# Attention's output projection: weights loaded and split ahead, its last column tile held back, the last LayerNorm moved into the MLP's streams

## The chip, the cores and the metric

The kernel runs on one core of a Trainium2 chip. The metric is device time in microseconds (us) of one execution. The time before is the median of three runs. The profile is that of one more execution, whose own time is given below beside its span (from its first to its last instruction).

## What is computed

Two post-norm transformer layers over 1024 latent tokens and 256 context tokens of width 1024, all in fp32. Layer 0 is a retention and gated-linear-attention mixer, layer 1 a windowed attention; each ends in a squared-ReLU MLP. The change lies in layer 1. Cut to that:

```python
q, k, v = split_cols(h @ w, (ATT_QW, ATT_KVW, ATT_KVW))        # 16 query heads, 4 key/value heads, width 64
q, k = axial_rope(q), axial_rope(k)
# each block of 128 queries: a softmax over the keys with |i-j| <= 128, all 256 context keys and a sink logit
y = merge_heads(window_attention(q, k, v, k_c, v_c, od_sink[j])) @ od_w_out[j]     # the output projection
x = layer_norm(ALPHA * x + g1 * y)                                                # over the 1024 features
x = layer_norm(ALPHA * x + g2 * (relu((x * (1 + sc2) + sh2) @ mlp_w1) ** 2 @ mlp_w2))
```

## The kernel before

Activations lie with features on the 128 partitions and tokens in the free dimension; `accs[1]` and `accs[2]` hold 512 latent tokens each, as eight tiles of 128 features. A product in fp32 is made of three matmuls of halves (`mm3`): weight and activation are each split into a rounded high part and a low remainder, and high*high, high*low and low*high are summed in PSUM.

A weight is split by `wsplit` (L246 to L253): SP's queue loads a 128x1024 fp32 tile `raw` (three buffers), ACT casts it to the high part (L251), and POOL, or DVE where `eng` says so, subtracts to get the low part (L252). The pair lies in one tile of the tag `w`, of which the pool `wg` has five.

Attention is a loop over 32 groups `u`: eight query blocks `n`, four key/value heads `g`, each with four query heads. For one head, `scores` (L1353 on) writes the scores into one of two PSUM tiles `pS`; DVE takes the row maximum (L1381, L1382) and ACT the exponentials `E` with their sums (L1385). `dens` makes the reciprocals of the denominators and puts them on diagonals `dg` (POOL, L1398). `turn` transposes the E of four heads for one key block on PE into one of two PSUM tiles `pE`, and copies them to `Et` (ACT at L1410, DVE at L1408 for the third key block); the tile of the first four `Et` is of the tag `w` too. `pv` sums E times v into `pO`, `end` multiplies the denominators in (L1429, L1430) and splits the result into `yh` (ACT, L1432) and `yl` (DVE, L1433). A group has five key blocks inside the sequence and four at its two ends. The loop is a software pipeline: while the E of group `u` are turned, the scores of group `u+1` are made.

The output projection of a finished pair of blocks (256 tokens) is the generator `residual`, which calls `w_out_steps` (L746 on): eight column tiles, each with one weight pair, 24 matmuls into the single PSUM tile `pW`, and one DVE update of `accs` (L758). With `halves` it yields after 12 and after 24 matmuls. The loop advances it twice in a group, so that a column tile falls into each group from `u` = 8 on: first half after the second turn, second half after the last scores. `wsplit` is called where the first half begins. The projection of the last two blocks (t = 9) comes after the loop, in whole column tiles into `pE`, with POOL and DVE taking turns at the subtractions. `norm` is the LayerNorm of a finished stretch of 256 tokens, advanced once per group; it shares `pW` (its mean stays there for the four subtractions of L712). After the projections for t = 7 and t = 9, `make_h` writes the modulated, split MLP input of 256 tokens of `accs[1]` into `yall`, over the attention output that was just used. `residual` also loads 1 MB of the stream into `accs` by SP's queue, behind a small POOL copy (L1324, L1325).

The last stretch, `accs[2][:, :, 256:512]`, has its LayerNorm `ln_` as a generator of ten steps. Nine of them run before the MLP; the tenth, and the four steps of the MLP input made from it, are the second stream of `Early`, which `mlp` advances after each up and each down product of its first weight block, by the rates given to `Early`; `need` runs a stream dry where the MLP reads it.

Order: within attention, PE's instructions of the loop are chained in program order (`TE.kept`), except `end` of the last group, the norms and what follows the loop. All else is ordered by a planner that simulates the program and takes, for each engine, what is ready with the earliest place in the program; so a cast can stand on ACT earlier than in the program. Each engine then works through its list in order.

Of the kernel before, what the change touches and what calls it, by code (L numbers as in the profile page):

```python
# [9 lines left out]
F32 = mybir.dt.float32  # L10
F32R = mybir.dt.float32r
# [3 lines left out]
ALU = mybir.AluOpType  # L15
# [4 lines left out]
P = 128  # L20
KT = 8
T = 1280
NT = 10
# [11 lines left out]
def backbone(ctx: ExitStack, tc: tile.TileContext, xT, cin, wmod, bmod, lng, lnb, w1, w2,  # L35
# [4 lines left out]
    def pool(**kw):  # L40
        if kw.get("space") is not DRAM:
            kw["reuse_waits"] = "tile"
        return tc.tile_pool(**kw)

    V, S, G, SY = nc.vector, nc.scalar, nc.gpsimd, nc.sync
# [27 lines left out]
    rawp = ctx.enter_context(pool(name="rawp", bufs=3))  # L73
# [5 lines left out]
    def nm(s):  # L79
        uid[0] += 1  # L80
        return f"{s}_{uid[0]}"
# [149 lines left out]
    def adv(gen, n):  # L231
        for _ in range(n):
            if next(gen, "end") == "end":
                return
# [11 lines left out]
    def wsplit(pool, src, eng=None):  # L246
        raw = rawp.tile([P, 1024], F32, tag="raw", name=nm("raw"))
        SY.dma_start(raw, src)
        both = pool.tile([P, 2, 1024], F32R, tag="w", name=nm("w"))
        hi, lo = both[:, 0, :], both[:, 1, :]  # L250
        S.copy(hi, raw)  # L251
        (eng or G).tensor_tensor(lo, raw, hi.bitcast(F32), ALU.subtract)  # L252
        return hi, lo  # L253
# [8 lines left out]
    def mm3(pt, wh, wl, xh, xl, start, stop):  # L262
        TE.matmul(pt, lhsT=wh, rhs=xh, start=start, stop=False)
        TE.matmul(pt, lhsT=wh, rhs=xl, start=False, stop=False)
        TE.matmul(pt, lhsT=wl, rhs=xh, start=False, stop=stop)
# [24 lines left out]
    def first_load(q):  # L290

        raws = []
        for k in range(0, KT, 2):
            raw = b1.tile([P, 2, 2, 256], F32, tag=("E0", "Ei0", "E1", "Ei1")[k // 2], name=nm("raw"), bufs=1)
            for a in range(2):
                SY.dma_start(raw[:, a], wmod[0, (k + a) * P:(k + a + 1) * P, 0:2048]
                             .rearrange("p (b c) -> p b c", b=2)[:, :, q * 256:q * 256 + 256])
            raws.append(raw)
        return raws
# [31 lines left out]
    def t16(name):  # L331
        return b1.tile([P, 16], F32, tag=name, name=name, bufs=1)
    u = t16("u")
# [24 lines left out]
    raws = first_load(0)  # L358
# [26 lines left out]
    with es_b1:  # L385
# [20 lines left out]
        for q in range(4):  # L406
            first_mods(q, raws)
            x_ = xs
            if q < 3:
                raws = first_load(q + 1)  # L410
# [138 lines left out]
    wg = ctx.enter_context(pool(name="wg", bufs=5, side="right"))  # L549
# [196 lines left out]
    def w_out_steps(y, wsrc, wp, acc, l, j, pW, engs=(None, None), wnext=None, halves=False):  # L746

        n = acc.shape[2]
        yh, yl = y
        for u in range(KT):  # L750
            wh, wl = [w.rearrange("p (k m) -> p k m", k=KT) for w in (wnext() if wnext else wsplit(wp, wsrc[u], engs[u % 2]))]
            pt = pW()
            for k in range(KT):
                xh, xl = [y_[k // 4][:, k % 4, :] if isinstance(y_, list) else y_[:, k, :] for y_ in (yh, yl)]
                mm3(pt[:, :n], wh[:, k, :], wl[:, k, :], xh, xl, k == 0, k == KT - 1)
                if halves and k == 3:
                    yield
            V.scalar_tensor_tensor(acc[:, u, :], pt[:, :n], gta[:, l, 0, u, j:j + 1], acc[:, u, :],  # L758
                                   op0=ALU.mult, op1=ALU.add)
            yield  # L760
# [5 lines left out]
    pSc, pO, pR, pW, pL = ring(2, 3), ring(0, 1), ring(4), ring(5, 7), ring(6)  # L766
# [9 lines left out]
    with pool(name="b3", bufs=1) as b3:  # L776
# [32 lines left out]
        def wnext():  # L809
            while len(ahead) <= n_ahead:  # L810
                src = next(srcs, None)
                if src is None:
                    break
                ahead.append(wsplit(wg, *src))
            return ahead.pop(0)
# [27 lines left out]
        def out_of(p_, y):  # L843
            return w_out_steps(y, wo0, wg, acc_of(p_)[0], 0, acc_of(p_)[1], pW, wnext=wnext)
# [31 lines left out]
        for tp_ in range(NT // 2):  # L876
# [20 lines left out]
            for t in (2 * tp_, 2 * tp_ + 1):  # L897
# [21 lines left out]
                for h in range(4):  # L919
                    en = V  # L920
# [91 lines left out]
        end = out_of(NT // 2 - 1, (yh, yl))  # L1012
# [106 lines left out]
    def new_h(hp, ci, l, mp, os_=(0, 256), los=(V, G)):  # L1119

        if ci not in hs:
            hs[ci] = h_tiles(hp, ci)
        return [((ci, o), h_steps(accs[ci][:, :, o:o + 256], l, 1, cj(ci), hs[ci][0][:, :, o:o + 256],
                                  hs[ci][1][:, :, o:o + 256], mp, "hf", 2, los=los)) for o in os_]

    es_h = ExitStack()
    hp = es_h.enter_context(pool(name="hp0", bufs=1))
    xd = [dram(f"xd{c}", [P, KT, CH[c][1]]) for c in range(3)]
    with pool(name="m0", bufs=1) as mp:
        ln_ = layer_norm_steps(accs[2][:, :, 256:512], 0, 0, mp, "ln_s", "ln_q", 1, True, pL, 512)  # L1130
        early = Early([new_h(hp, 1, 0, hp, (0,), (V, V)) + new_h(hp, 1, 0, hp, (256,)) + new_h(hp, 2, 0, hp, (0,)), [(None, ln_)] + new_h(hp, 2, 0, hp, (256,))], ((2, 2), (2, 2)))
# [38 lines left out]
        rest = mlp(0, [0, 1, 2], hs, accs, wg, mp, post, chain(*[mod_sums(1, s_, mp, pM) for s_ in range(3)]), tick, ticks0, early)  # L1170
# [24 lines left out]
    pS, pE, pO, pW = bank2("S2", 1024, 2), bank2("E2", 512, 2), bank2("O2", 512, 1), bank2("W2", 512, 1)  # L1195
# [38 lines left out]
    todo = None  # L1234
    for grp in range(3):
# [19 lines left out]
        for i in range(4):  # L1255
            src = wkv[i] if grp == 0 else wq[4 * (grp - 1) + i]
            wu.append(wsplit(wg, src, V if i % 2 else G))
        for t in range(0 if grp == 0 else 2, NT):
# [30 lines left out]
            todo = nxt  # L1289
# [14 lines left out]
    with pool(name="p2", bufs=1) as p2:  # L1304
# [3 lines left out]
        def get_v(t):  # L1308
            if t not in vts:
                v_ = p2.tile([P, 256], F32, tag="vc" if t < 2 else "vl", name=nm("v"), bufs=2 if t < 2 else 4)  # L1310
                SY.dma_start(v_, vTd[t])
                vts[t] = v_
            return vts[t]
# [2 lines left out]
        G.memset(ones_c, 1.0)  # L1316
        get_v(0)
        get_v(1)
        def residual(y, t, ci):
            o0 = (t - 1) * P - CH[ci][0]  # L1320
            if o0 == 0:
                accs[ci] = new_acc(acp, ci)
            asl = accs[ci][:, :, o0:o0 + 256]
            G.tensor_copy(asl[:, 0, 0:1], first[0])  # L1324
            SY.dma_start(asl, xd[ci][:, :, o0:o0 + 256])  # L1325
            yield from w_out_steps(y, wo1, wg, asl, 1, 0, pW if t < NT - 1 else pE, (None, None) if t < NT - 1 else (None, V), halves=t < NT - 1)
            if t in (NT - 3, NT - 1):
                make_h(accs[1][:, :, o0:o0 + 256], 1, 1, 0, *[y_[:, :, o0:o0 + 256] for y_ in yall], p2, "ln_q", 1)

# [8 lines left out]
        rest, norms = iter(()), iter(())  # L1338
# [98 lines left out]
        todo = [(n, g) for n in range(8) for g in range(4)]  # L1437
# [5 lines left out]
        for u, (n, g) in enumerate(todo):  # L1443
            nk, _, dens, turn, pv, end = nxt
            nxt = group(*todo[u + 1]) if u + 1 < len(todo) else None
            dens()
            for kk in range(nk):
                turn(kk)
                if nxt and kk < 3:
                    nxt[1](kk)  # L1450
                if kk == 1:
                    adv(rest, 1)
            if nxt:
                nxt[1](3)
            adv(rest, 1)
            for kk in range(nk):
                pv(kk)
            end()
            TE.kept = False
            adv(norms, 1)  # L1460
            TE.kept = u + 1 < len(todo)
            if g == 3 and n % 2 == 1:
                adv(rest, 1000)
                if n > 1:
                    adv(norms, 1000)
                    norms = norm(n, chunk_of(n))
                rest = residual([y_[:, :, (n % 4) * P - P:(n % 4) * P + P] for y_ in yall], n + 2, chunk_of(n + 2))
        for _ in rest:
            adv(norms, 1)
        adv(norms, 1000)  # L1470
    if stop == "x3":
# [10 lines left out]
    with pool(name="hp1", bufs=1) as hp, pool(name="m1", bufs=1) as mp:  # L1482
        hs = {1: yall}
        ln_ = layer_norm_steps(accs[2][:, :, 256:512], 1, 0, mp, "ln_s", "ln_q", 2, True, pL, 512, True)
        early = Early([new_h(hp, 2, 1, mp, (0,)), [(None, ln_)] + new_h(hp, 2, 1, mp, (256,))], ((4, 4), (4, 4)))
        adv(ln_, 9)

        pend = []

        def post(ci, o0, n):  # L1490
            c0 = CH[ci][0] - 256 + o0

            def store(k, kn):
                (SY if k % 4 else S).dma_start(out[:, k:k + kn, c0:c0 + n], accs[ci][:, k:k + kn, o0:o0 + n])

            g_ = layer_norm_steps(accs[ci][:, :, o0:o0 + n], 1, 1, mp, "ln_s", "ln_q", 2, True, pL, 512, store)
            while next(g_) != "free":
                pass
            while pend:
                adv(pend.pop(), 100)  # L1500
            pend.append(g_)

        post(*mlp(1, [1, 2], hs, accs, wg, mp, post, early=early))
        adv(pend.pop(), 100)
# [102 lines left out]
```

## Time and profile before

| | |
|---|---|
| median of 3 runs | 3048.98 us (3047.06 to 3050.82) |
| the profiled execution's own time | 3047.85 us |
| its span | 3046.1 us |
| PE (TensorE, matmuls) busy | 2871.2 us, 94% of the span |
| PE's weight loads busy | 2414.7 us, 79% |
| DVE (VectorE) busy | 1660.5 us, 55% |
| ACT (ScalarE) busy | 981.1 us, 32% |
| POOL (GpSimd) busy | 811.0 us, 27% |
| mean granted TensorE clock | 0.978 of full speed |

PE is busy nearly all of the time, so a stage gets shorter by what PE waits less in it, or by a higher granted clock. Row texts: start, duration, engine, line, operation, output<-inputs, shapes, count; in square brackets how long the engine was idle just before, and on what it waited.

### The profile page before, as it was taken

The numbers are of one execution on the slowest core, as the hardware profiler recorded it, in microseconds if no ns is written. First come the engines' busy times: TensorE is split into PE (matmuls) and PEld (weight loads), VectorE is DVE, ScalarE is ACT, GpSimd is POOL, SyncE is SP. The second block draws the span as 40 slices with busy tenths as digits, with TensorE's granted clock in tenths as the row PEclk, the third lists the DMA queues.
The fourth block names the chain that finished last, engine by engine and source line by source line (L and its number), as shares of the span: only waits on it lengthen the run. The fifth ranks groups of instructions, "written<-read, shape, count | busy, mean of one in ns | idle before, by whom it ended". The sixth has DMA issues, their size and how long they took to land. (4 is left out here: it accounts for less than half of the span.)

```text
span 3046.1 us, 42253 instructions
## 1 busy us (share of the span) xinstructions
PE 2871.2 (94%) x17204; PEld 2414.7 (79%) x17204; DVE 1660.5 (55%) x2709; ACT 981.1 (32%) x1628; POOL 811.0 (27%) x610
## 2 busy tenths in 40 slices
PE   7989998999999999999999998888888999999997
PEld 4867888888888888888888776676677888888886
DVE  3754478777765444444445546666765434343445
ACT  4434344444211211112113515545543221112113
POOL 3120245544311111111112512323344221222121
PEclk9999999999999999999999999999889999999999
DMA  7377675652222222222201472221221111111111
GB/s 252 111 235 240 205 268 180 202 185 97 71 72 70 66 66 76 69 74 70 65 19 44 154 191 71 66 79 58 63 96 50 56 49 36 55 56 49 36 41 56
DMA packets 168353, 304.44 MB, mean 100 GB/s; under 512 B 13504, under 2 KB 98752, under 8 KB 167648
## 3 DMA queue, kind: packets, MB, share of 16 engines
q1 hardware_dynamic: 149744, 272.91, 27.7%
q0 software_dynamic: 6480, 16.26, 2.0%
q10 hardware_dynamic: 11936, 12.59, 1.5%
q8 instruction: 135, 2.21, 0.3%
q14 instruction: 58, 0.48, 0.1%
HBM read 257.67 MB, written 44.04 MB: 99 GB/s over the span
## 5 line engine op out<-in xcount | busy, mean ns | idle before, releaser
L252 POOL TENSOR_TENSOR w<-raw,w 128x1024 fp32r<-128x1024 f32 x210 | 508.6, 2430 | 1545.3 <-ACT w L251 1504.5
L62 PE MATMUL k<-hh,w 128*128 128x256 f32 (+1 forms) x3264 | 826.3, 339 | 4.8 <-DVE hh L259 3.4
L62 PE MATMUL k<-uh,w 128*128 128x512 f32 (+1 forms) x2816 | 763.7, 352 | 7.3 <-DVE acc L1064 6.9
L1064 DVE SCALAR_TENSOR_TENSOR acc<-k,gta,acc 128x512 f32<-128x512 f32 (+1 forms) x704 | 441.4, 648 | 566.8 <-PE k L62 559.0
L62 PEld LDWEIGHTS k<-hh,w 128*128 128x128 f32 x3264 | 569.5, 192 | 82.6 <-issue 13.1
L62 PEld LDWEIGHTS k<-uh,w 128*128 128x128 f32 x2816 | 501.2, 189 | 88.2 <-DVE acc L1064 14.6
L62 PE MATMUL k<-hl,w 128*128 128x256 f32 (+1 forms) x1632 | 554.6, 340 | 8.6 <-POOL hl L260 7.2
L62 PE MATMUL k<-ul,w 128*128 128x512 f32 (+1 forms) x1408 | 494.7, 351 | 0.0
L251 ACT CAST w<-raw 128x1024 fp32r<-128x1024 f32 x260 | 269.0, 1048 | 694.8 <-PE k L62 460.7
L62 PEld LDWEIGHTS k<-hl,w 128*128 128x128 f32 x1632 | 312.5, 192 | 48.4 <-POOL hl L260 8.9
L62 PEld LDWEIGHTS k<-ul,w 128*128 128x128 f32 x1408 | 266.1, 189 | 36.2 <-issue 0.8
L1046 ACT ACTIVATE r<-k 128x512 f32<-128x512 f32 (+1 forms) x176 | 90.8, 516 | 613.6 <-PE k L62 613.2
L62 PE MATMUL k<-yh,w 128*128 128x256 f32 (+1 forms) x1088 | 271.3, 335 | 8.1 <-DVE acc L758 8.1
L62 PEld LDWEIGHTS k<-yh,w 128*128 128x128 f32 x1088 | 191.8, 196 | 30.0 <-DVE acc L758 9.3
L181 DVE SCALAR_TENSOR_TENSOR k<-raw,cs,k 128x256 f32<-128x256 f32 (+1 forms) x168 | 96.6, 575 | 160.8 <-DMA raw<-in_wmod 158.7
L62 PE MATMUL k<-yl,w 128*128 128x256 f32 (+1 forms) x544 | 180.9, 333 | 0.0
L1049 DVE TENSOR_TENSOR r<-r 128x1024 f32<-128x1024 f32 (+1 forms) x88 | 109.9, 1249 | 69.0 <-ACT uh L1048 68.9
L62 PE MATMUL pW<-yh,w 128*128 128x256 f32 x384 | 91.0, 317 | 55.8 <-POOL w L252 42.9
L62 PE MATMUL pS<-kall,qt 128*128 128x256 f32 (+1 forms) x512 | 126.8, 360 | 8.6 <-ACT E L1385 8.1
L736 POOL TENSOR_SCALAR acc<-acc,lg_t,lb_t 128x256 f32<-128x256 f32 x124 | 103.6, 847 | 98.6 <-DVE acc L730 50.8
L1381 DVE TENSOR_REDUCE sm<-pS 128x1 f32<-128x640 f32 (+1 forms) x128 | 100.7, 788 | 42.1 <-PE pS L62 40.7
L1385 ACT ACTIVATE E<-pS,sm 128x640 f32<-128x640 f32 (+1 forms) x128 | 98.7, 771 | 70.8 <-DVE sm L1382 70.1
(276 smaller groups left out, 3778.7 us busy)
## 6 DMA issues: line engine op xcount, KB each, us to landing
raw<-in_w SPq DMA_DIRECT2D x128, 512.0 KB, 3.4
raw<-in_wo SPq DMA_DIRECT2D x72, 512.0 KB, 3.5
raw<-in_wmod SPq DMA_DIRECT2D x128, 256.0 KB, 2.7
raw<-in_wfm SPq DMA_DIRECT2D x48, 512.0 KB, 5.4
raw<-in_wmod SPq DMA_DIRECT2D x32, 512.0 KB, 4.3
kt<-kd SPq DMA_DIRECT2D x20, 512.0 KB, 5.6
qt<-qT POOLq DMA_DIRECT2D x32, 256.0 KB, 3.0
qT<-qT ACTq DMA_DIRECT2D x30, 256.0 KB, 3.4
```

What stands on the lines that cost most here:

```text
L62: return self.put(nc.tensor.matmul(*a, **kw))
L181: V.scalar_tensor_tensor(dst, src, cs[:, k + a, j:j + 1], dst, op0=ALU.mult, op1=ALU.add)
L251: S.copy(hi, raw)
L252: (eng or G).tensor_tensor(lo, raw, hi.bitcast(F32), ALU.subtract)
L736: G.tensor_scalar(acc[:, k, :], acc[:, k, :], lg_t[:, l, s, k:k + 1], lb_t[:, l, s, k:k + 1], op0=ALU.mult, op1=ALU.add)
L1046: S.activation(rf[:, i, :n], pts[i][:, :n], AF.Relu)
L1049: V.tensor_tensor(rf[:, :, :n], rf[:, :, :n], rf[:, :, :n], ALU.mult)
L1064: V.scalar_tensor_tensor(a_, pt[:, :n], gta[:, l, 1, m, cj(ci):cj(ci) + 1], a_, op0=ALU.mult, op1=ALU.add)
L1381: V.tensor_reduce(sm_[:, 0, i:i + 1], sall, AX.X, ALU.max)
L1385: S.activation(E_[:, :256 + L], sall, AF.Exp, scale=0.125, bias=sm_[:, 1, i:i + 1], accum_out=sm_[:, 3, i:i + 1])
```

## The change

The weights of all 32 column tiles go into one list, with the engine of their subtraction. `w_load` starts the load of the next one, `w_prep` casts and subtracts the oldest loaded one, `ready` holds the pairs. A group calls `w_load` before `dens` from `u` = 5 on and `w_prep` between the last scores and `pv` from `u` = 6 on; `residual` takes its pairs from `ready`. Column tiles still fall into groups 8 to 31, but the last group no longer advances the projection (`part` is 0): the eighth column tile for t = 7 comes after `end` of the last group. After the loop each turn of the while loop loads and splits one more. The nine steps of `ln_` before the MLP are gone; its stream starts with all ten steps, at five steps a call where it was four.

```diff
+        wsrcs = [(wo1[u], V if t == 3 and u % 2 else G) for t in range(4) for u in range(KT)]
+        raws, ready = [], []
+        def w_load():
+            if wsrcs:
+                raw = rawp.tile([P, 1024], F32, tag="raw", name=nm("raw"))
+                src, en = wsrcs.pop(0)
+                SY.dma_start(raw, src)
+                raws.append((raw, en))
+        def w_prep():
+            if raws:
+                raw, en = raws.pop(0)
+                both = wg.tile([P, 2, 1024], F32R, tag="w", name=nm("w"))
+                S.copy(both[:, 0, :], raw)
+                en.tensor_tensor(both[:, 1, :], raw, both[:, 0, :].bitcast(F32), ALU.subtract)
+                ready.append((both[:, 0, :], both[:, 1, :]))
...
-            yield from w_out_steps(y, wo1, wg, asl, 1, 0, pW if t < NT - 1 else pE, (None, None) if t < NT - 1 else (None, V), halves=t < NT - 1)
+            yield from w_out_steps(y, wo1, wg, asl, 1, 0, pW if t < NT - 1 else pE, wnext=lambda: ready.pop(0),
+                                   halves=t < NT - 1)
...
+            part = 1 if u + 1 < len(todo) else 0
+            if u > 4:
+                w_load()
             dens()
             for kk in range(nk):
                 turn(kk)
                 if nxt and kk < 3:
                     nxt[1](kk)
                 if kk == 1:
-                    adv(rest, 1)
+                    adv(rest, part)
             if nxt:
                 nxt[1](3)
-            adv(rest, 1)
+            adv(rest, part)
+            if u > 5:
+                w_prep()
             for kk in range(nk):
                 pv(kk)
...
-        for _ in rest:
+        while True:
+            w_load()
+            w_prep()
+            if next(rest, "end") == "end":
+                break
             adv(norms, 1)
...
-        early = Early([new_h(hp, 2, 1, mp, (0,)), [(None, ln_)] + new_h(hp, 2, 1, mp, (256,))], ((4, 4), (4, 4)))
-        adv(ln_, 9)
+        early = Early([new_h(hp, 2, 1, mp, (0,)), [(None, ln_)] + new_h(hp, 2, 1, mp, (256,))], ((4, 5), (4, 5)))
```

## Rows read from the trace of the kernel before

**Rows 1.** Stages: window, length, PE, PEld, DVE, ACT, POOL busy, PEclk, DMA share, GB/s.
```profile
1860.50:1919.00 58.50, 52.56 (x409) 38.84 (x409) 40.31 (x102) 40.03 (x93) 12.03 (x31) 1.00 0.16 48
1919.00:2243.30 324.30, 273.05 (x2013) 224.96 (x2009) 219.49 (x409) 164.36 (x356) 104.21 (x146) 0.93 0.21 65
...
2350.00:2400.00 50.00, 50.00 (x247) 42.46 (x246) 15.56 (x24) 9.01 (x11) 9.55 (x4) 1.00 0.14 46
```
**Rows 2.** Waits from 1919 to 2243: us in total, times, longest.
```profile
PE pW L62 <- POOL w L252: 40.2, 21, 2.1
PE pW L62 <- ACT ln_q L714: 5.4, 1, 5.4
```
**Rows 3.** PE's timeline: each group's last matmuls, for some groups.
```profile
1918.88 0.60 PE L62 MATMUL pO<-dg,ones_c 128*64 128x256 f32 x4
1933.46 0.60 PE L62 MATMUL pO<-dg,ones_c 128*64 128x256 f32 x4
1946.49 0.60 PE L62 MATMUL pO<-dg,ones_c 128*64 128x256 f32 x4
...
2069.88 0.60 PE L62 MATMUL pO<-dg,ones_c 128*64 128x256 f32 x4
2088.14 0.60 PE L62 MATMUL pO<-dg,ones_c 128*64 128x256 f32 x4
...
2186.26 0.60 PE L62 MATMUL pO<-dg,ones_c 128*64 128x256 f32 x4
2203.57 0.60 PE L62 MATMUL pO<-dg,ones_c 128*64 128x256 f32 x4
2215.48 0.60 PE L62 MATMUL pO<-dg,ones_c 128*64 128x256 f32 x4
...
2242.70 0.60 PE L62 MATMUL pO<-dg,ones_c 128*64 128x256 f32 x4
2258.08 0.60 PE L62 MATMUL pO<-dg,ones_c 128*64 128x256 f32 x4
```
**Rows 4.** Timeline inside the group that ends at 1946.49.
```profile
1935.17 1.05 ACT L251 CAST w<-raw 128x1024 fp32r<-128x1024 f32 x1
...
1936.30 2.35 POOL L252 TENSOR_TENSOR w<-raw,w 128x1024 fp32r<-128x1024 f32 x1 [0.65 <-ACT w L251]
...
1936.49 0.28 PE L62 MATMUL pW<-yl,w 128*128 128x256 f32 x1
...
1936.56 2.37 DVE L1433 TENSOR_TENSOR yl<-yf,yh 128x256 fp32r<-128x256 f32 x1
...
1938.70 0.51 PE L62 MATMUL pW<-yh,w 128*128 128x256 f32 x2 [1.93 <-POOL w L252]
...
1938.86 0.81 DVE L1381 TENSOR_REDUCE sm<-pS 128x1 f32<-128x640 f32 x1
...
1940.64 0.69 DVE L1408 COPY Et<-pE 128x512 f32<-128x512 f32 x1 [0.73 <-PE pE L65]
...
1941.16 1.04 PE L65 MATMUL pE<-ident,E 128*128 128x128 f32 x8
```
**Rows 5.** PE alone, 3 us after the next group's wait, columns as in rows 1.
```profile
1951.70:1954.70 3.00, 2.97 (x15) 0.57 0.57 175
```
**Rows 6.** The tile yl in attention: durations in ns, smallest, median, largest.
```profile
L1433 DVE TENSOR_TENSOR yl<-yf,yh x31: 361/2371/2376, 1860.6 to 2246.1; 128x256 fp32r<-128x256 f32 x31
```
**Rows 7.** ACT's timeline in the last group.
```profile
2245.59 2.96 ACT L251 CAST w<-raw 128x1024 fp32r<-128x1024 f32 x3
```
**Rows 8.** PE's waits from 2258 to 2345.
```profile
PE k L62 <- ACT ln_s L693: 5.8, 1, 5.8
PE pE L62 <- ACT yh L1432: 4.6, 1, 4.6
PE k L62 <- DVE acc L758: 3.2, 1, 3.2
```
**Rows 9.** POOL's timeline at the MLP's start.
```profile
2298.07 4.40 POOL L736 TENSOR_SCALAR acc<-acc,lg_t,lb_t 128x256 f32<-128x256 f32 x6 [1.19 <-DVE acc L730]
```

## The prediction

> **What bounds the kernel now.** Read the busy shares of the table above first, then the stages, then what PE waits for in the stage of the change. PE is the engine that bounds: after attention the MLP holds it at 50.0 of 50 us at full clock [rows 1], so whatever ends earlier before the MLP ends the kernel earlier by as much. The projection's groups, 1919.0 to 2243.3, are different: PE is busy 273.1 of 324.3 us at a granted clock of 0.93 [rows 1]. Of the 51 us idle, 40.2 are 21 waits of at most 2.1 us for POOL's weight subtraction, and one wait of 5.4 us is for the LayerNorm that shares pW [rows 2].
>
> A group shows how the wait comes about. The cast of the weight runs on ACT at the group's start, 1935.17 for 1.05 us, then POOL's subtraction from 1936.30 for 2.35 us. PE stands before the third matmul of the column tile until 1938.70 [rows 4]. Ends of successive groups lie 14.58 and 13.03 us apart [rows 3]: the same instructions, but in the longer one the clock falls after the wait, to a mean of 0.57 over 3 us, so most of that stretch at 1.2 GHz instead of 2.4 [rows 5]. A stretch at half clock costs 14.58 - 13.03 = 1.55 us. Seven groups without a LayerNorm wait take 14.56 to 14.64 us; the other such groups 11.9 to 13.7.
>
> **The change part by part. Weights ahead, 23 groups (u = 8 to 30).** A pair is needed two groups after its split. Cast and subtraction take 1.05 + 2.35 us [rows 4] of 11 or more, so the wait for w goes. What it costs on PE is taken from start to start: the matmul before the wait starts at 1936.49, the next at 1938.70 [rows 4], 2.21 us apart. Without a wait it would be 0.12: 247 matmuls of 512 columns take 50 us in the MLP [rows 1], 0.20 each, and I count 0.12 for 256 columns. So the wait costs 2.09 us. Floor of a group: 13.03 - 2.09 = 10.94 us. Loads, casts and subtractions are as many as before; the two pairs prepared in groups 6 and 7 add 2 x 1.05 us on ACT and 2 x 2.35 us on POOL, busy 40 and 12 of 58.5 us there [rows 1], and I count nothing for them. SP issues each load a group earlier, behind at most one wait for the 1 MB load of accs; two groups of slack cover that.
>
> What is late next? The subtraction does not vanish; it stays once per group, and it blocks DVE. yl takes 361 ns at least and 2371 ns in the median [rows 6]; in the group shown it starts 0.26 us into POOL's subtraction and ends 0.28 us after it [rows 4]. Where will the planner put the cast now? In the last group three casts run back to back, two of them for tiles that stand after the loop in the program [rows 7]: it pulls casts forward as far as the tiles of tag w allow, and their order in that ring is the same as before (Et, pair, Et, pair). I therefore expect cast, subtraction and the 2.37 us yl at the same place of the group. DVE's next row maximum then starts 4.8 us into the group (1938.86, the group before having ended at 1933.46 + 0.60, [rows 3, 4]) and takes 0.81; with some 0.2 for the small operation behind it and the 0.69 us copy of the third Et [rows 4], pE is free again 6.6 us into the group, with the signal to PE 6.7. PE needs that tile for the fifth turn, the last four of the eight transposes that start at 1941.16 [rows 4], so about 1941.5, 7.4 us into the group; without the 2.09 us it gets there at 5.3. That is a new wait of 1.4 us, and behind it stand the scores of the last head, which need E from the same delayed maximum. A group then takes 10.94 + 1.4 = 12.3 us. Bounds: 10.94 if subtraction and yl fall apart; 13.0 if the whole 2.1 us return. I take 12.3, nearest to the row as it stands.
>
> The Trainium skill (SBUF — State Buffer, Who interferes with whom) states that a VectorE instruction with two SBUF inputs and a GpSimd instruction that reads SBUF exclude each other, and that the one that starts second is blocked until the first has ended. The rows agree for the order they show, 2371 against 361 ns. By that rule it would be enough that yl starts first: POOL would lose 0.4 us, DVE nothing, and the sum would be that of rival 1 below.
>
> Sum for the groups: 17 groups of five key blocks x 12.3 = 209.1; three of four key blocks x 11.2 (11.91 in [rows 3], less 2.09, plus 1.4) = 33.6; three with a LayerNorm's hold of pW, which the change leaves: 18.26 (2069.88 to 2088.14) becomes 10.94 + 5.4 = 16.3, 17.31 (2186.26 to 2203.57) about 15.6, and the third about 14. Together 288.6 against 2242.70 - 1918.88 = 323.8: **-35 us**. The half-clock stretches are in it as gone, since the groups before the projection, with PE idle 5.9 of 58.5 us, have a clock of 1.00 [rows 1].
>
> **Last column tile past the last group.** The last group takes 15.38 us [rows 3], with two waits for w and ACT busy for 2.96 us with three casts [rows 7] between copies of Et. A group of four key blocks has a floor of 11.91 - 2.09 = 9.8; without the column tile (24 x 0.12 = 2.9) and without scores of a next group it is under 6.9, but a chain of turns, copies and pv with nothing beside it: I take 7 (5 if nothing disturbs, 9 with the LayerNorm's operations on ACT). The column tile costs its 2.9 us behind it. -15.4 + 7 + 2.9 = **-5.5**. PE's 4.6 us wait for yh [rows 8] is gone: from the end of pO to yl takes 2.5 us in the group shown (1936.56 against 1934.06, [rows 3, 4]), under the 2.9, and make_h, whose ACT operations stood before that cast, now stands behind it. **-4.6**, and **-1.5** for a stretch at half clock, which I expect behind a wait of that length. make_h of the first half comes some us later; it has the 23 us of the t = 9 projection (8 x 2.9) as cover, and if that were gone the MLP's first product would wait for it.
>
> **Last LayerNorm inside the MLP.** It removes the 3.2 us in which its sums wait for the last update [rows 8], and PE starts the MLP at once. But the second product needs make_h of the second half, a chain through one buffer that stands behind POOL's LayerNorm scaling (4.40 us for six, [rows 9]); the 5.8 us wait [rows 8] is mostly that chain, which starts with the end of the projection in either kernel. So most of 3.2 comes back: I take **-1** (bounds -4 and 0). Against it, all ten steps and four of the MLP input now lie between the first product and the fourth of the first block; I add **+2** (0 if PE's products cover them, +10 if the 5.8 and 3.2 us waits [rows 8] come up again there).
>
> Sum: -35.2 - 5.5 - 4.6 - 1.5 - 1 + 2 = -45.8. The profiled execution took 3047.85 us, 1.75 more than its span; 3047.85 - 45.8 = **3002 us**. The median shown, 3048.98, is 1.1 above it, well inside the range.
>
> **The rivals.** (1) Subtraction and yl fall apart. For it: in the program w_prep stands behind the last scores, and ACT is idle there. Against: rows 7. Then 17 x 10.94 + 3 x 9.8 + (16.3 + 15.6 + 12.5) = 259.8, -64, and with the tail's -10.6: 2973 us.
>
> (2) The new waits keep the clock swinging. For it: half clock after 2 us of idle in about half of the groups. Against: 1.00 in the groups before the projection [rows 1], though PE idles there too. Ten stretches x 1.55 = 15.5 less gain: 3018 us. The Trainium skill (TensorE: Matmul & The Clock Gate, A second HAM failure mode: psum-queue depth-cycling) describes short idles of PE between groups of matmuls that make its clock swing and cost throughput; by that rule this case would happen here. The rows show it behind waits of 2 us in half of the groups, and show no wait of 1.4 us.
>
> (3) Nothing is gained: the planner had the pairs as early as the ring allows, and they stay late. Against: in program order they are two groups apart. 3046 us, within what can be told from no change.
>
> (4) Slower: a cast stands on ACT waiting for its tile. The ring of five holds one or two Et and now up to three pairs; a pulled-forward cast whose tile is still held by the pair in use would wait for the second half of that column tile, late in the group, and E and Et queue behind it on ACT. For it: rows 7, the planner's habit. Against: three pairs and one Et leave a fifth tile, and the planner sees this wait. It decides from (64 + 10.6)/23 = 3.2 us of such waiting per group beyond the floor; at 5 us: 3047.85 - 74.6 + 115 = 3088 us.
>
> **How the numbers follow.** Forecast 0.50, rival 1 0.30, rival 2 0.10, rival 3 0.03, rival 4 0.07. 3002 us is the likeliest; its own range is 2988 to 3016 (group of 11.8 to 12.8 us, tail at its bounds). Low end 2964: rival 1 with the tail at its best. High end 3024: rival 2 with the LayerNorm's +10. Outside remain rivals 3 and 4 and little else. A measurement of this kernel tells 0.2% (6 us) from no change; faster 0.90, same 0.03, slower 0.07.
>
> **What would show it.** Right: no wait of PE for w between 1919 and the loop's end; groups of 12 to 12.6 us with about 1.4 us before the fifth turn, on DVE's copy of Et; yl still near 2.37 us; no wait on yh after the loop. Groups near 11 us with yl at 0.4 mean rival 1; groups alternating by 1.5 us at a clock under 0.95 rival 2; ACT idle on a weight tile rival 4. Wrong altogether if PE's waits for w stay, or if the MLP's first block takes up more than 10 us of what attention gives.

## The result, and the profile after

The changed kernel takes 3013.42 us (median of four executions, 3010.48 to 3020.45) against 3048.02 us for the kernel before beside it: ratio 0.9891, 95% interval 0.9869 to 0.9912. It is faster, by 35 us, at the slow end of the likeliest case's own range (2988 to 3016). The profiled execution is the slowest of the four (3020.45 us, span 3018.6), so stages are compared below, each from its own start. The engines' busy shares, from the page:

```profile
PE 2863.4 (95%) x17204; PEld 2403.4 (80%) x17204; DVE 1662.4 (55%) x2709; ACT 978.9 (32%) x1628; POOL 808.1 (27%) x610
```

The stages of the change, with the columns of [rows 1]: the groups without the projection (1 to 7), groups 8 to 30, the last group, and the projection's last part.

```profile
1865.14:1923.64 58.50, 51.28 (x378) 36.97 (x376) 40.74 (x94) 37.59 (x86) 16.94 (x33) 0.97 0.13 37
1931.60:2221.90 290.30, 256.66 (x2013) 209.47 (x2009) 216.71 (x407) 162.84 (x356) 105.72 (x146) 0.98 0.23 73
2221.90:2227.90 6.00, 6.00 (x49) 4.40 (x47) 5.60 (x7) 4.41 (x8) 2.48 (x5) 1.00 0.00 1
2227.90:2264.40 36.50, 29.27 (x208) 28.37 (x207) 29.51 (x42) 16.39 (x23) 25.77 (x17) 0.86 0.36 130
```

The same 2013 matmuls of groups 8 to 30 stand in 290.3 us instead of 324.3 [rows 1], and the clock there has gone from 0.93 to 0.98. The ends of groups, in PE's timeline (compare [rows 3]):

```profile
1905.07 0.60 PE L62 MATMUL pO<-dg,ones_c 128*64 128x256 f32 x4
1917.83 0.60 PE L62 MATMUL pO<-dg,ones_c 128*64 128x256 f32 x4
1931.51 0.60 PE L62 MATMUL pO<-dg,ones_c 128*64 128x256 f32 x4
1943.61 0.60 PE L62 MATMUL pO<-dg,ones_c 128*64 128x256 f32 x4
```

Groups 6 and 7 now take 12.76 and 13.68 us; group 8 takes 12.10, and so do nearly all behind it, with none of the alternation of 14.58 and 13.03 [rows 3]. PE's waits from 1860 to 2400 (us in total, times, longest):

```profile
PE pE L65 <- DVE Et L1427: 20.1, 19, 1.1
PE pS L62 <- ACT E L1404: 11.8, 13, 2.8
PE pW L62 <- DVE acc L712: 10.1, 2, 5.4
PE k L62 <- ACT r L1046: 10.0, 1, 10.0
PE pE L62 <- DVE acc L758: 6.6, 2, 5.1
PE k L62 <- DVE acc L1064: 1.0, 3, 0.5
PE pW L62 <- DVE ln_s L703: 0.6, 1, 0.6
```

The 40.2 us of waits for POOL's w [rows 2] are gone from the list, and so is the wait for yh [rows 8]. The first line is new: 19 waits of 1.06 us on DVE's copy of Et. It is the wait that the prediction put in their place, as the timeline of group 8 shows (compare [rows 4]):

```profile
1933.21 1.05 ACT L1333 CAST w<-raw 128x1024 fp32r<-128x1024 f32 x1
1934.35 2.40 POOL L1334 TENSOR_TENSOR w<-raw,w 128x1024 fp32r<-128x1024 f32 x1 [0.68 <-ACT w L1333]
1934.60 2.43 DVE L1452 TENSOR_TENSOR yl<-yf,yh 128x256 fp32r<-128x256 f32 x1
1936.95 0.81 DVE L1400 TENSOR_REDUCE sm<-pS 128x1 f32<-128x640 f32 x1
1937.92 0.68 DVE L1427 COPY Et<-pE 128x512 f32<-128x512 f32 x1
1938.66 0.66 PE L65 MATMUL pE<-ident,E 128*128 128x128 f32 x4 [1.08 <-DVE Et L1427]
...
1941.40 2.38 PE L62 MATMUL pO<-Et,v 128*64 128x256 f32 x20
```

POOL subtracts a weight that nobody waits for yet, but yl starts 0.25 us behind it and ends 0.28 us behind it, the row maximum and the copy of Et start late, and PE meets the copy. Over all of attention yl is as slow as it was in [rows 6] (ns: smallest, median, largest):

```profile
L1452 DVE TENSOR_TENSOR yl<-yf,yh x32: 360/2416/2428, 1865.3 to 2231.5; 128x256 fp32r<-128x256 f32 x32
```

The stretch in which the change does not deliver is behind the last group (the timeline of all engines, cut to the chain):

```profile
2230.29 7.16 POOL L736 TENSOR_SCALAR acc<-acc,lg_t,lb_t 128x256 f32<-128x256 f32 x6
2237.41 1.29 POOL L260 TENSOR_TENSOR yl<-hf,yh 128x512 fp32r<-128x512 f32 x1
2238.74 1.09 ACT L378 ACTIVATE hf<-acc,mod,osc 128x256 f32<-128x256 f32 x2 [3.80 <-POOL yl L260]
2239.86 2.51 DVE L259 CAST yh<-hf 128x512 fp32r<-128x512 f32 x1 [3.39 <-ACT hf L378]
2243.23 0.47 DVE L758 SCALAR_TENSOR_TENSOR acc<-pE,gta,acc 128x256 f32<-128x256 f32 x1
2243.75 0.58 PE L62 MATMUL pE<-yh,w 128*128 128x256 f32 x1 [5.05 <-DVE acc L758]
...
2282.09 0.58 PE L62 MATMUL k<-yh,w 128*128 128x256 f32 x1 [10.00 <-ACT r L1046]
```

PE stands 5.05 us until 2243.75 for pE's update, 1.55 us until 2258.90 for the same again, and 10.0 us before the MLP's second product. Behind the 5.05 us it runs at half clock until about 2252, as the same matmul shows just before and just after:

```profile
2251.75 0.41 PE L62 MATMUL pE<-yl,w 128*128 128x256 f32 x1
2252.28 0.28 PE L62 MATMUL pE<-yl,w 128*128 128x256 f32 x1
```

Stage by stage, in us, worked out from the starts of those ones_c matmuls: groups 1 to 5, 6 and 7, 8 to 30, the last group, "tail" from its end to the MLP's first activation r of 512 columns, and the rest of the span. The kernels e1 to e12 are the experiments of the next section. The first column, the end of group 0, lies in code that no kernel changes.

| kernel | group 0 ends | 1–5 | 6, 7 | 8–30 | last | tail | rest |
|---|---|---|---|---|---|---|---|
| before | 1858.20 | 42.25 | 18.43 | 323.82 | 15.38 | 98.09 | 689.93 |
| after | 1862.84 | 42.23 | 26.44 | 289.86 | 5.98 | 101.94 | 689.31 |
| e1_ahead_only | 1863.92 | 42.21 | 23.84 | 289.86 | 7.53 | 102.80 | 689.84 |
| e2_ahead_hold | 1856.63 | 42.22 | 23.85 | 289.38 | 5.99 | 102.69 | 689.84 |
| e3_change | 1857.98 | 42.21 | 22.16 | 289.31 | 5.98 | 101.61 | 689.35 |
| e4_yl_pool | 1855.14 | 41.61 | 18.19 | 261.78 | 5.52 | 102.34 | 689.32 |
| e9_sub_dve | 1862.83 | 42.25 | 23.88 | 281.48 | 5.99 | 99.71 | 689.36 |
| e6_mh_dve | 1856.34 | 42.22 | 22.15 | 290.26 | 5.98 | 101.85 | 689.10 |
| e8_yl_pool_pm | 1866.42 | 41.58 | 18.19 | 252.31 | 5.52 | 103.39 | 689.19 |
| e10_all | 1860.69 | 41.60 | 18.20 | 252.29 | 5.52 | 103.62 | 689.58 |
| e11_tail_dve | 1863.88 | 42.22 | 22.15 | 290.44 | 5.98 | 95.34 | 689.09 |
| e12_pool_tail_dve | 1864.40 | 41.58 | 18.20 | 260.05 | 5.52 | 96.76 | 689.09 |

Two things are to be seen in it. The unchanged start varies by 11 us between profiled executions (1855 to 1866), so a span hides a gain of a few us that a stage shows. And from the end of group 0 the changed kernel gains 32.1 us, where the sum of the prediction had 45.8.

### The profile page after: what moved, and what is told of

Same layout as the page of the kernel before. It is cut to its first block, busy times and chain, and to the rows that moved or that the text cites. A ratio compares the mean times of both kernels' runs of the same rounds, so it can differ in the third digit from the quotient of the medians.

```text
span 3018.6 us, 42215 instructions
## 1 busy us (share of the span) xinstructions
PE 2863.4 (95%) x17204; PEld 2403.4 (80%) x17204; DVE 1662.4 (55%) x2709; ACT 978.9 (32%) x1628; POOL 808.1 (27%) x610
## 5 line engine op out<-in xcount | busy, mean ns | idle before, releaser
L252 POOL TENSOR_TENSOR w<-raw,w 128x1024 fp32r<-128x1024 f32 x182 | 439.4, 2423 | 1518.2 <-ACT w L251 1457.9
L251 ACT CAST w<-raw 128x1024 fp32r<-128x1024 f32 x228 | 235.8, 1047 | 694.2 <-PE k L62 471.5
L62 PE MATMUL k<-yh,w 128*128 128x256 f32 (+1 forms) x1088 | 271.9, 336 | 21.2 <-DVE acc L758 11.2
L62 PE MATMUL pS<-kall,qt 128*128 128x256 f32 (+1 forms) x512 | 124.5, 355 | 13.8 <-ACT E L1404 13.3
L736 POOL TENSOR_SCALAR acc<-acc,lg_t,lb_t 128x256 f32<-128x256 f32 x124 | 102.3, 839 | 103.0 <-DVE acc L730 56.8
L65 PE MATMUL pE<-ident,E 128*128 128x128 f32 x608 | 96.5, 284 | 21.1 <-DVE Et L1427 20.1
```

Source lines behind the costliest of these rows:

```text
L62: return self.put(nc.tensor.matmul(*a, **kw))
L65: return self.put(nc.tensor.transpose(*a, **kw))
L736: G.tensor_scalar(acc[:, k, :], acc[:, k, :], lg_t[:, l, s, k:k + 1], lb_t[:, l, s, k:k + 1], op0=ALU.mult, op1=ALU.add)
```

## The experiments

Each result is a median, its ratio to the kernel before run beside it, and the 95% interval of that ratio. The first four ran together (before: 3053.03 us).

**e1: weights ahead alone.** The held last step and the moved LayerNorm are undone.

```diff
-            part = 1 if u + 1 < len(todo) else 0
+            part = 1
-        early = Early([...], ((4, 5), (4, 5)))
+        early = Early([...], ((4, 4), (4, 4)))
+        adv(ln_, 9)
```

> Only the first part of the change: pairs loaded three and split two groups ahead; the last group advances the projection again, and nine steps of the last LayerNorm run before the MLP again. Theory: the weights ahead carry nearly all. Groups 8 to 30 at 12.1 us as in the changed kernel, groups 6 and 7 about 8 us longer than before together, the last group about 10.5 us instead of 15.4 because its two waits for w go, PE's wait for yh after the loop still 4 to 5 us. Sum -34 + 8 - 5 = -31 us, 3012 to 3020 us. Rival: the held-back column tile and the moved LayerNorm carry 8 us or more of the gain; then this run is above 3021 us.

3020.09 us, ratio 0.9895 [0.9879, 0.9912], at the edge between the theory's range and the rival's. Most of the gain is the weights ahead, 33 us by the medians where the whole change (e3, below) has 39: groups 8 to 30 are as short as in the change. Three parts of the expectation missed. Groups 6 and 7 are 5.4 us longer than before, not 8. The last group is 7.53 us without holding anything back, not 10.5, so 7.85 of its 9.4 us come from the earlier weights too. And PE's wait for yh is 1.0 us, not 4 to 5: it went with the earlier weights, before anything was held back.

**e2: weights ahead and the step held back; e3: the change again.** e2 undoes the LayerNorm's move alone (the last three lines above).

> The change without its third part: pairs ahead and the last column tile held back, but nine steps of the last LayerNorm before the MLP, at four steps a call. Theory: the move of the LayerNorm is worth nothing, since the MLP's second product waits for the split input of the second half (10.0 us in the changed kernel, 3.2 + 5.8 before): within 3 us of the changed kernel, the 10.0 us wait parted again in about 3 and 6. Rival: the move gives back the 3.2 us: 3 to 5 us slower than the changed kernel.

> The changed kernel once more, beside the others on the same chip: 3013 us, 3008 to 3020. Its groups 8 to 30 at 12.1 us.

3015.82 us, 0.9885 [0.9867, 0.9903], and 3013.74 us, 0.9877 [0.9858, 0.9896]. The intervals of e1, e2 and e3 overlap, so times do not part them. The stages do: the hold takes 1.5 us off the last group and 0.1 off the tail, and the LayerNorm 0.8 to 1.1 us off the tail. The 10.0 us of the change part again in e2, into 5.8, 2.6 and 1.3 (expected: about 3 and 6). Two profiles of one kernel, after and e3, differ by 4.3 us in groups 6 and 7.

**e4: attention's yl subtraction on POOL,** behind the weight's subtraction, in every group but the last. If the two block each other when they stand on two engines, one engine should be better.

```diff
-                V.tensor_tensor(yall[1][...], yf, ysl.bitcast(F32), ALU.subtract)
+                (V if (n, g) == (7, 3) else G).tensor_tensor(yall[1][...], yf, ysl.bitcast(F32), ALU.subtract)
```

> The changed kernel with the subtraction that makes yl on POOL instead of DVE, but for the very last group. Theory: in the changed kernel each group loses 1.06 us before the fifth turn because yl stands 2.4 us on DVE beside POOL's weight subtraction, and the row maximum and the copy of the third Et behind it. With yl behind the weight subtraction on POOL they cannot meet: groups 8 to 30 at 10.9 to 11.1 us, 20 x 1.1 = 22 us less, groups 6 and 7 some 6 us less together, 2985 us (2980 to 2995). Rival: ACT makes the wait, with the 1.05 us cast ahead of E and the Et copies: groups stay at 12.1 us, 3013 us. Second rival: POOL's list gets late (its diagonals dg stand behind yl) and end waits for dg: groups at 12 us or more with PE waiting for POOL.

2974.55 us (2970.86 to 2980.98), 0.9748 [0.9732, 0.9763]: 39 us less than the change, and less than the 2980 to 2995 expected. The stages of the two profiles from the end of group 0 on hold 31.9 us of it, 27.5 in groups 8 to 30 and 4.0 in groups 6 and 7; no stage explains the rest, which is within the spread of the executions. The yl row and PE's waits of that run:

```profile
L1452 POOL TENSOR_TENSOR yl<-yf,yh x31: 718/729/748, 1857.4 to 2178.8; 128x256 fp32r<-128x256 f32 x31
```

```profile
PE k L62 <- ACT r L1046: 10.0, 1, 10.0
PE pW L62 <- DVE acc L712: 8.2, 2, 5.4
PE pS L62 <- ACT E L1404: 6.2, 11, 1.2
PE pE L62 <- DVE acc L758: 5.8, 1, 5.8
```

The 20.1 us on Et are gone, groups take 10.82 us and groups 6 and 7 9.1 each: both losses had this cause. POOL's yl is twice as long as the fastest on DVE (729 against 360 ns), and no wait of PE is for it.

The next four ran together (before: 3050.2 us).

**e9: weight subtractions on DVE,** the other way to have both on one engine.

```diff
-        wsrcs = [(wo1[u], V if t == 3 and u % 2 else G) for t in range(4) for u in range(KT)]
+        wsrcs = [(wo1[u], V) for t in range(4) for u in range(KT)]
```

> The changed kernel with all 32 weight subtractions on DVE instead of POOL; yl stays on DVE. It tells whether a group's 1.06 us wait comes from DVE being shut out by POOL or from DVE having too much to do. DVE gets 1.2 us more work of its own per group and loses the 2.0 us in which yl stands. Theory (shut out): yl at 0.4 us, no wait or a smaller one before the fifth turn, groups at 10.8 to 11.6 us, 2990 to 3005 us. Rival (load): DVE's row maxima and Et copies come later still, groups at 12.5 us or more, 3020 us or more.

3007.24 us, 0.9847 [0.9829, 0.9864]; groups of 11.65 us. yl, and then the largest of PE's waits from 1860 to 2400:

```profile
L1452 DVE TENSOR_TENSOR yl<-yf,yh x32: 359/416/421, 1865.3 to 2219.0; 128x256 fp32r<-128x256 f32 x32
```

```profile
PE pS L62 <- ACT E L1404: 25.0, 29, 2.3
```

yl never takes 2.4 us with no subtraction on POOL beside it, which shows the blocking from its other side. But each subtraction now stands in DVE's queue for 1.22 us. In one group it starts at 1990.01, between a row maximum that ends at 1990.05 and the small operation L1401 behind it, which E needs and which starts only at 1991.48; PE then waits 0.57 us for E. The groups and the time come out a little above the expected 10.8 to 11.6 and 2990 to 3005 us, between e4 and the change and far from the rival's.

**e6: make_h's lower halves behind attention on DVE,** to take POOL's part (the yl of L260, behind the LayerNorm scaling L736) out of the tail's chain.

```diff
-                make_h(accs[1][...], 1, 1, 0, ..., p2, "ln_q", 1)
+                make_h(accs[1][...], 1, 1, 0, ..., p2, "ln_q", 1, None, (V, V))
```

> The changed kernel with the low halves of both make_h calls of attention wholly on DVE (half of them were on POOL). Theory: after the loop PE waits 5.05 us for DVE's update L758, because on DVE a cast of make_h stands ahead of it, which waits for ACT, which waits for POOL's low half behind 7.2 us of LayerNorm scaling; the 10.0 us before the MLP's second product have the same cause a second time. Without POOL in the chain the first wait falls to 1 us or less and the second to 3 to 6: 6 to 11 us less, 3002 to 3008 us. Rival: DVE itself is late there, from LayerNorm sums and casts blocked by POOL's weight subtractions; then less than 3 us comes of it, 3011 us or more.

3014.69 us, 0.9887 [0.9869, 0.9906], no gain. The first wait fell from 5.05 to 0.31 us and the one before the MLP's second product from 10.0 to 5.6, but the tail is as long as it was, since new waits came between them, the longest of 6.43 us (the timeline, then SP's own waits from 2206 to 2242):

```profile
2219.90 11.87 POOL L736 TENSOR_SCALAR acc<-acc,lg_t,lb_t 128x256 f32<-128x256 f32 x8
2231.73 2.52 POOL L1334 TENSOR_TENSOR w<-raw,w 128x1024 fp32r<-128x1024 f32 x1
...
2237.96 1.04 ACT L1333 CAST w<-raw 128x1024 fp32r<-128x1024 f32 x1 [8.94 <-DMA raw<-in_wo]
...
2240.27 2.24 DVE L1334 TENSOR_TENSOR w<-raw,w 128x1024 fp32r<-128x1024 f32 x1 [7.84 <-ACT w L1333]
2243.03 0.47 DVE L758 SCALAR_TENSOR_TENSOR acc<-pE,gta,acc 128x256 f32<-128x256 f32 x1
2243.64 0.55 PE L62 MATMUL pE<-yh,w 128*128 128x256 f32 x1 [6.43 <-DVE acc L758]
```

```profile
SPq L1326 <- POOL w L1334: 16.9, 2, 13.9
```

Read from below: SP could not issue a weight load for 13.9 us, because the subtraction that frees its buffer stood on POOL behind eight scalings. The cast waits for that load, DVE's subtraction for the cast, and the update L758 is queued behind that subtraction. The expectation's rival held in the time, but not for its reason: DVE was not full, it stood idle for 7.84 us.

**e8: the mean of layer 1's LayerNorms copied out of PSUM by ACT,** on top of e4, so that pW is free earlier in the three groups with a LayerNorm. **e10: e4, e6 and e8 together.**

```diff
         pm = mean(pp, 0)
+        if l == 1 and not pe_sums:
+            S.copy(sm[:, 0, :], pm[:, :n])
+            pm = sm[:, 0, :]
```

> yl on POOL as in the run before, and the LayerNorm's mean copied from pW to SBUF by ACT as soon as it is there, so that pW is free for the projection. Theory: the groups of 19.3 and 16.6 us wait 5.4 and some 4 us for pW; with the copy (0.4 us) they wait 1 us or less: 7 to 10 us less than with yl on POOL alone, 2965 to 2968 us. Rival: the four subtractions now have two SBUF inputs and are shut out by POOL, the LayerNorm gets later and its end delays what follows: no gain or a loss, 2973 us or more.

> All three together: yl on POOL, make_h's low halves on DVE, the mean copied out of pW. If the three waits are independent the gains add: -39 measured for yl on POOL, 6 to 11 and 7 to 10 expected for the others, 2955 to 2963 us. If they share DVE or POOL time after the loop, the sum stays 5 us or more behind: above 2963 us.

2972.62 us, 0.9739 [0.9721, 0.9758], and 2973.83 us, 0.9747 [0.9733, 0.9761]; both miss what the theories said (2965 to 2968 and 2955 to 2963). Groups 8 to 30 lose 9.5 us against e4, and two of the three LayerNorm groups fall to about 13 us (19.31 to 13.27, 16.61 to 13.14). The tail gives 1 us back, and neither median can be told from e4's 2974.55. The net 8 us of the stages are so neither confirmed nor excluded by the times, whose intervals are some 11 us wide; the span does not help, since the unchanged start of e8's profile is 11 us later than e4's.

The last two ran together (before: 3051.74 us).

**e11: e6, and all eight weight subtractions of the projection's last part (t = 9) on DVE,** so that none stands behind L736. **e12: e11 and e4 together.**

```diff
-        wsrcs = [(wo1[u], V if t == 3 and u % 2 else G) for t in range(4) for u in range(KT)]
+        wsrcs = [(wo1[u], V if t == 3 else G) for t in range(4) for u in range(KT)]
```

> The changed kernel with the lower halves of make_h behind attention on VectorE, and with all eight weight subtractions of the last row of query blocks (t = 3) on VectorE instead of every second one. In the run with make_h alone, the wait of 5.05 us fell to 0.31, but PE then waited 6.43 us for VectorE's update L758, which stood behind a subtraction, which stood behind a cast, which waited 8.94 us for its load; SP had waited 13.9 us to issue loads because POOL's subtraction, which frees the load's buffer, stood behind 11.87 us of LayerNorm scaling (L736). Theory (POOL's scaling holds the load buffers): no subtraction stands behind the scaling, SP's longest wait on a subtraction falls under 8 us, the 6.4 us falls under 2, the stretch from the last group's end to the MLP's first activation falls from 101.9 to 98 us or less, and the time is 3 to 6 us below the changed kernel's of the earlier comparison as a ratio: 0.9858 to 0.9869 of before. Rival (VectorE is full there, whatever holds the loads): waits of PE on VectorE's acc and ln_s stay at 6 us or more in total, the stretch is 100.5 us or more, ratio 0.9875 to 0.989.

> The same two edits, with attention's yl subtraction on POOL as well (except in the last group). Groups 8 to 30 stay near 262 us. Theory (POOL's scaling holds the load buffers): the stretch behind the last group falls from 102.3 us to 98 or less, ratio 0.9725 to 0.9738 of before (0.9748 with yl on POOL alone). Rival (VectorE is full there): the stretch is 101 us or more and the ratio 0.9745 to 0.976.

e11: 3011.36 us, 0.9866 [0.9849, 0.9882]. Its waits of PE from 1860 to 2400, for the tail:

```profile
PE k L62 <- ACT r L1046: 10.4, 1, 10.4
...
PE pW L62 <- DVE ln_s L721: 2.2, 1, 2.2
PE pE L62 <- DVE acc L758: 1.4, 2, 1.1
```

and its last two casts for the projection, in ACT's timeline (the last group ends at 2224.67, in e6 at 2216.95):

```profile
2237.38 1.05 ACT L1333 CAST w<-raw 128x1024 fp32r<-128x1024 f32 x1 [1.09 <-DMA raw<-in_wo]
2240.57 1.06 ACT L1333 CAST w<-raw 128x1024 fp32r<-128x1024 f32 x1 [2.14 <-DMA raw<-in_wo]
```

The 6.4 us have become 1.4, and the tail 95.34 us instead of 101.9, while POOL's scaling takes as long as before (11.72 us for eight). The last two casts start 12.7 and 15.9 us behind the last group, in e6 21.0 and 22.2. The clock is 1.00 in the first 40 us of this tail, where two of the change's first four stretches of 10 us have 0.73 and 0.76. So POOL's place in the queues is what the projection's last part waited for, in two ways: through make_h's lower halves, and through the load buffers behind its subtractions. Taking out the first alone (e6) gained nothing. The second alone is nearest in e9, whose weight subtractions are all on DVE while make_h is unchanged: its tail is 99.71 us, some 2 us shorter. The wait before the MLP's second product stays, 10.4 us; no run takes POOL's scaling itself out of its chain. One part of the expectation missed: SP's longest wait for a subtraction from 2214 to 2250 is 11.3 us and not under 8, now for one on DVE. The time's interval holds the rival's ratio too; the stage decides between them.

e12: 2977.22 us, 0.9748 [0.9728, 0.9768]. Its tail is 96.76 us, 5.6 below e4's, but the time is the rival's: the gain of the stage is not seen in the median, as with e8.

The versions with yl on POOL (e4, e8, e10, e12) are the best, 2973 to 2977 us by the medians of three comparisons, and cannot be ordered among themselves.

## Why the prediction was right, and where its sum was off

**The groups.** The forecast was 288.6 us for groups 8 to 30; it took 289.9. The step with a wait in place of the one removed came as put: a group of 12.10 us (12.3), a wait of 1.06 us before the fifth turn (1.4) on DVE's Et, yl at 2.4 us. e4 and e9 show its cause, since either way of putting the two subtractions on one engine makes the wait for Et go. The four-key-block groups took 10.6 to 10.8 (11.2), those with a LayerNorm 18.97, 15.90 and 17.31 (16.3, 14 and 15.6), so the ordinary groups gained nearly what the LayerNorm's lost.

**The rivals.** Rival 1 (yl and the subtraction fall apart, 2973 us) did not happen, but e4 makes it happen by hand and takes 2974.55: groups of 10.82 us against the floor of 10.94 in the text. The Trainium skill (SBUF — State Buffer, Who interferes with whom) says that issue order decides which of the two blocks. The trace agrees: in all 23 groups where yl meets the subtraction, POOL starts first, by 0.25 to 0.64 us, and yl is the one held up. Behind the last group the other order occurs once, with another DVE instruction of two SBUF inputs 0.02 us ahead, and there it is POOL's subtraction that takes 3.46 us instead of 2.4:

```profile
2226.82 1.22 DVE L730 TENSOR_TENSOR acc<-acc,ln_s 128x1024 f32<-128x1024 f32 x1
2226.84 3.46 POOL L1334 TENSOR_TENSOR w<-raw,w 128x1024 fp32r<-128x1024 f32 x1 [3.32 <-ACT w L1333]
```

Rival 2: the clock is 0.98 over groups 8 to 30 and 1.00 over the eleven of them before the first LayerNorm wait (1931.6 to 2064.6), so waits of 1.06 us did not make it swing there. By the Trainium skill (TensorE: Matmul & The Clock Gate, A second HAM failure mode: psum-queue depth-cycling) it would have; the trace disagrees, except in groups 6 and 7 of the profiled execution (below). The half clock that the text saw "in about half of the groups" before was in seven of twenty by its own count. Rivals 3 and 4: no wait for w is left, and ACT's waits in groups 8 to 30 hold none of a cast for its tile.

**Failed: "I count nothing" for groups 6 and 7.** Their two pairs cost 8.0 us in the profiled execution (26.44 against 18.43) and 3.7 in e3's. The price was put on ACT and POOL, which have room. The trace shows it on DVE: the pair's subtraction stretches yl there as well, and without projection matmuls between, PE meets the delayed E and Et sooner, 0.98, 0.98 and 0.44 us in group 6. With yl on POOL (e4) the two groups are at 18.19 us again. In the profiled execution a stretch at half clock comes behind those waits:

```profile
1908.42 2.12 DVE L1452 TENSOR_TENSOR yl<-yf,yh 128x256 fp32r<-128x256 f32 x1
1909.54 0.61 PE L62 MATMUL pS<-kall,qt 128*128 128x384 f32 x2 [0.98 <-ACT E L1404]
1911.93 0.66 PE L65 MATMUL pE<-ident,E 128*128 128x128 f32 x4 [0.98 <-DVE Et L1427]
1913.03 0.61 PE L62 MATMUL pS<-kall,qt 128*128 128x384 f32 x2 [0.44 <-ACT E L1404]
1913.93 4.07 PE L62 MATMUL pO<-Et,v 128*64 128x256 f32 x20
```

The last line's are the same 20 matmuls that take 2.38 us in group 8. The text argues the stretched yl just so for the groups behind, and did not apply it to these two. In e3's profile group 6 has the same three waits (0.97, 0.98 and 0.44 us), takes 11.08 us instead of 12.76 and shows no such stretch; what decides between the two is open.

**Failed: "-4.6" for the yh wait and "-1.5" for the half clock behind it.** The tail was to be 2.2 us shorter, with the held tile's 2.9 us, and is 3.9 us longer. The wait for yh did go, though by e1 the earlier weights took it away and not the held tile. The half clock did not go: it comes behind the 5.05 us instead, for some 8 us. What the step missed is what is late next: the chain over POOL's scaling, make_h and DVE's in-order queue, 5.05 and 1.55 us, with the clock at 0.86 in that part. The text let make_h come "some us later" with 23 us of cover, and looked at its own end, the MLP's first product; it did not look at what stands behind make_h on DVE, the update that frees pE. e11 takes POOL's subtractions out of both chains and its tail is 95.3 us, where the sum had 98.1 - 2.2 = 95.9.

**The last LayerNorm** was put at +1 (-1 and +2) and is -1 by e2 against e3. Of the 3.2 us wait most came back, as forecast: 10.0 us now stand before the MLP's second product where 5.8, 3.2 and POOL's 2.6 stood around it.

The account from the end of group 0: 8.0 (groups 6 and 7) + 6.1 (tail) + 1.3 (groups 8 to 30) - 1.0 (last group, 5.98 for 7) - 0.6 (rest) = 13.8 us, the difference between 45.8 and 32.1 but for rounding. In e3's profile groups 6 and 7 cost 4.3 us less than that.

So the mechanism forecast for the groups held, and two steps beside it failed, both to the same side. That the time still lies in the range is owed to the range's width. The ends of the ranges do not come out of the text's own terms to better than a few us: rival 1 with the tail at its best is 2973 - 7 = 2966 (2964 in the text), rival 2 with the LayerNorm's +10 is 3017.5 + 8 = 3025.5 (3024), and groups and tail at their bounds give 2985 to 3023 (2988 to 3016). The result lies inside by either.

## What to carry to other kernels

When a stall is removed by doing its work earlier, the work still stands somewhere: look at which other engine it blocks there, not only at whether its own engine has room. If two elementwise operations with two SBUF inputs block each other on DVE and POOL, put both on the engine that is off the critical chain, even if one takes twice as long there. An in-order queue makes a late helper everyone's problem: follow the instruction behind it, and the buffer that it frees, before calling it covered.

## What was not expected of the hardware

The fp32 to fp32r cast on DVE (128x512, one input) takes 0.41 us where it is fastest, and 2.51 us at 2239.86, where it runs beside POOL's subtraction (2239.74 to 2242.08): here an instruction with one SBUF input is held up as well. The Trainium skill (SBUF — State Buffer, Who interferes with whom) allows this for casts in a two-port mode; which mode ran is not in the trace. DVE's row maxima from PSUM keep their 0.82 us beside such a subtraction (in e4 one starts at 1993.75, inside POOL's of 1993.50 to 1995.90).
